# A hybrid encoder layer in split single precision: where the low halves of the weights, the scan's decay factors and a 64-row matmul are made

## The chip, the cores and the metric

One core of a Trainium2 chip runs the whole program. The metric is device time in microseconds (us) of one execution; of the kernel before there are three timed executions, and one more that carried a profile. TensorE is PE in the profile and its weight loads are PEld; VectorE is DVE, ScalarE is ACT, GpSimd is POOL, and SP is the engine that issues most transfers.

## What is computed

One layer of a streaming encoder on 544 tokens (512 of a prompt, 32 of a second request with caches), model width 1024:

```
h = rmsnorm(x); [q,k,v | z,xBC,dt | gate_a,gate_b] = h @ w_in
A: q, k normed per head; attention over a band with a clipped relative-position bias
B: xBC -> causal conv -> silu; chunked state-space scan (SSD) in 4 groups of 8 heads:
     seg   = acs[i] - acs[j]                  # acs: running sum of the decay exponents
     decay = exp(seg) for i >= j, else 0
     y     = ((C B^T) * decay) @ dx  +  (C @ h_prev) * exp(acs)
     h     = h_prev * exp(last)  +  B^T @ wj
   y -> gated rmsnorm with silu(z)
x += (sigmoid(gate_a) * (A @ w_proj_a) + sigmoid(gate_b) * (B @ w_proj_b)) @ w_out
x += down(gelu(conv(u_g)) * conv(u_v)),  u = rmsnorm(x) @ w_up
x += sigmoid(rmsnorm(x) @ w_ple_gate) * (p @ w_ple)
```

Outputs are y, the new keys and values, the scan's states and the conv contexts.

## The kernel before

All tokens lie along the free axis, features on the 128 partitions. A product with a weight matrix runs in units: one unit is a 128x1024 block of weights (128 output features, 8 chunks of 128 input features). `unit_order` lists 194 units in a fixed order: the conv and scan inputs and z first, then q, k, v, the gates, the projections, the feed-forward part and the last gate.

Each product is made in three passes of a fast reduced format (float32r). A weight tile is split as hi = rounded weight, lo = weight - hi; the activations likewise. `mm3` (L273) issues, for one chunk, hi x hi, hi x lo and lo x hi, each in two halves of 272 tokens: 6 matmuls a chunk, 48 a unit. One chunk is the grain in which the order of work on PE is written by hand: `dense.run(n)` puts n chunks between the pieces of the scan and of the attention. PE's instructions run in just the order in which the code issues them (each is pinned behind the last one); on the other engines a list scheduler fixes the order when the program is built, and each engine then runs its list in order.

Weights come by `load` (L234), two units (1 MB) in one transfer on SP's queue. `prep` (L240) makes hi on ACT (L250) and lo as a subtraction (L254): on DVE, but for units below 40 with an odd number on POOL. The code calls `prep` one unit ahead (PF = 1); hi and lo have two buffers each, so hi of unit u+1 can only be written when PE has finished unit u-1.

Three stages follow from this order. Up to about 395 us the conv inputs, z and the first q, k, v are made, with the scan between them: 20 iterations (4 groups, 5 chunks of tokens) of `ssd_a` (L611: products and decay factors) and `ssd_b` (L663: outputs and the next state). In `ssd_a` the decay factors of 8 heads are made in two halves: for each of 4 heads DVE computes min(ab - acs, 0) (L651), then ACT takes the exponential of all 4 (L652), then DVE multiplies with the masked product cbm (L653), which was copied from PSUM to SBUF (L625). From 395 to 645 us the attention of 8 pairs of heads runs between dense chunks. For a pair, `stack` (L806) builds ks (k rounded, twice, on 128 rows) and qs (q rounded on 64 rows, q's remainder on the other 64), and kl, the remainder of k on the head's own 64 rows; `att_a` (L823) adds up two products for the logits, the first on 128 rows (L848) and the second on the 64 rows of kl (L849). From 645 us on there is dense work alone, with its epilogues.

Of the kernel before, what the change touches and what calls it, by code (L numbers as in the profile page):

```python
# [9 lines left out]
F32 = mybir.dt.float32  # L10
# [106 lines left out]
def trunk(ctx: ExitStack, tc: tile.TileContext, a):  # L117
# [57 lines left out]
    def spt(shape, tag, bufs):  # L175
        return pools["sp"].tile(shape, F32, tag=tag, name=tag, bufs=bufs)
# [23 lines left out]
    r0 = wp.tile([128, 2, 1024], F32, tag="wr", name="wr", bufs=2)  # L200
    for k, c0, c1 in ((1, 0, 256), (2, 256, 512), (4, 512, 1024)):
        for u in range(2):
            nc.sync.dma_start(r0[:, u, c0:c1], a["w"][0, :, u, c0:c1])
        while len(xt) <= k:
            load_x(len(xt))
# [22 lines left out]
    raws = {0: r0}  # L228
# [3 lines left out]
    PF = 1  # L232

    def load(j):  # L234
        if 2 * j < len(order) and j not in raws:
            r = wp.tile([128, 2, 1024], F32, tag="wr", name="wr", bufs=2)
            nc.sync.dma_start(r, a["w"][j])
            raws[j] = r

    def prep(u):  # L240
        if u >= len(order) or u in ready or u in used:
            return
        load(u // 2)
        r = raws[u // 2][:, u % 2, :]
        hi = wp.tile([128, 1024], F32R, tag="wh", name="wh", bufs=2)
        lo = wp.tile([128, 1024], F32R, tag="wl", name="wl", bufs=2)
        ready[u] = (hi, lo)
        if u < 2:
            return r
        cp = S.copy(hi, r)  # L250
        if u == 3:
            tc.add_manual_dep(cp.ins, first_rstd[0].ins.name, ORDER, reason="order")
        eng = G if u < 40 and u % 2 == 1 else V
        eng.tensor_tensor(lo, r, hi.bitcast(F32), op=SUB)  # L254
        load(u // 2 + 1)
# [8 lines left out]
    def next_unit(kind, k0, c0):  # L264
        u = pos[0]
        assert order[u] == (kind, k0, c0), (order[u], kind, k0, c0)
        pos[0] += 1
        for i in range(u, u + PF + 1):
            prep(i)
        used.add(u)  # L270
        return ready.pop(u)
# [149 lines left out]
    load(1)  # L421
# [129 lines left out]
    def bias_vector():  # L551
        er = const.tile([16, EROW], F32, name="er")
        nc.sync.dma_start(er[:, 383:EROW], a["rb"])
        V.tensor_scalar(er[:, 383:EROW], er[:, 383:EROW], -1.0, None, op0=MUL)
        V.tensor_copy(er[:, 0:383], er[:, 383:384].to_broadcast([16, 383]))
        nc.sync.dma_start(evec, er)
        for h in range(16):
            dense.defer(16 + 16 * h, lambda h=h: bias_rows(h))
# [52 lines left out]
    def ssd_a(g, c):  # L611
# [12 lines left out]
        cbm = spt([128, 128], "cbm", 2)  # L624
        V.tensor_tensor(cbm[:Q, :Q], sm[:Q, 0:Q], tri[:Q, :Q], op=MUL)  # L625
# [18 lines left out]
        for hh in range(2):  # L644
# [4 lines left out]
            for i in range(4):  # L649
                hd = 8 * g + 4 * hh + i  # L650
                V.tensor_scalar(m[:Q, i, :Q], ab[:Q, i, :Q], tm[:Q, 1, c, hd : hd + 1], 0.0, op0=SUB, op1=MIN)  # L651
            S.activation(m[:Q, :, :Q], m[:Q, :, :Q], AF.Exp)  # L652
# [151 lines left out]
    stk = {}  # L804

    def stack(m, hi):  # L806
# [5 lines left out]
        kl = st(512, "kl") if hi == 0 else stk[0][2]  # L812
# [10 lines left out]
    def att_a(m, i):  # L823
# [15 lines left out]
        for hi in range(2):  # L839
# [3 lines left out]
            if i == 0:  # L843
                PE.matmul(L[:, :n], lhsT=q[own, 0:n], rhs=k[own, 0:n], start=True, stop=True)
            else:
                qs, ks, kl = stk[hi]
                sl = slice(n - 256, n - 128)
                PE.matmul(L[:, :n], lhsT=qs[:, sl], rhs=ks[:, 0:n], start=True, stop=False)  # L848
                PE.matmul(L[:, :n], lhsT=qs[own, sl], rhs=kl[own, 0:n], start=False, stop=True)  # L849
# [297 lines left out]
    prev = None  # L1147
    att_load(0)
# [115 lines left out]
```

## Time and profile before

| | us |
|---|---|
| three timed executions | 1412.04, 1412.58 (median), 1417.83 |
| the profiled execution, its own time | 1413.28 |
| its span in the trace | 1411.2 |
| PE busy | 1376.0 (98%) |
| DVE busy | 916.0 (65%) |
| ACT busy | 613.4 (43%) |
| POOL busy | 352.1 (25%) |

The median of the timed executions and the profiled one differ by 0.7 us. Matmuls are pipelined, so a matmul's own duration (about 290 ns for 272 tokens) is much longer than its distance to the next (about 125 ns); gaps on PE shorter than the difference do not show as idle time. The granted TensorE clock over the whole span was 0.991 of full speed.

The profile says by itself in which stages PE has room: the share of busy time over the whole span mixes a stage in which DVE is nearly full with 755 us in which only PE is.

### The profile page before, as it was taken

How to read it: one execution, taken by the hardware profiler on the slowest of the kernel's cores; microseconds unless marked ns; L12 is line 12 of the kernel's file. 1: busy time of each engine (PE TensorE's matmuls, PEld its weight loads, DVE VectorE, ACT ScalarE, POOL GpSimd, SP SyncE). 2: the span in 40 equal slices, each digit the busy share in tenths (PEclk: the TensorE clock that was granted, in tenths of full speed). 3: DMA queues.
4: the chain of work that ended last, by engine and by line, in shares of the span. 5: the costliest groups of instructions: out<-in, count | busy, mean ns of one | idle time of the engine just before them, and what ended most of it. 6: DMA issues, size and time to landing. Idle time of an engine off the chain costs nothing.

```text
span 1411.2 us, 26759 instructions
## 1 busy us (share of the span) xinstructions
PE 1376.0 (98%) x11065; PEld 1324.1 (94%) x11065; DVE 916.0 (65%) x1654; ACT 613.4 (43%) x1016; POOL 352.1 (25%) x464
## 2 busy tenths in 40 slices
PE   7998898989999999999999999999999999999998
PEld 7997897989988888889999999999999999999998
DVE  7999999996865555564355334577777537753545
ACT  5444343455566666654244223344444214432342
POOL 5466475464422112210000000023333103310000
PEclk9999999999999999999999999999999999999999
DMA  5723232323443323311222332222222232222221
GB/s 175 241 90 109 87 120 64 116 92 110 132 138 114 103 88 99 103 64 61 90 91 90 122 122 90 91 78 79 85 88 91 90 106 90 91 93 90 90 90 65
DMA packets 41929, 142.16 MB, mean 101 GB/s; under 512 B 9264, under 2 KB 13248, under 8 KB 29520
## 3 DMA queue, kind: packets, MB, share of 16 engines
q1 hardware_dynamic: 41808, 140.46, 29.6%
q8 instruction: 87, 1.43, 0.4%
q14 instruction: 34, 0.28, 0.1%
HBM read 129.27 MB, written 14.31 MB: 102 GB/s over the span
## 4 chain that ended last, share of the span: by engine, by line
PE 81%; DVE 13%; DMA 2%; ACT 2%; issue 1%; POOL 1%; SPq 0%; POOLq 0%; ACTq 0%
PE dps L130 72%; DVE m L651 3%; PE L L130 3%; DVE cv L597 2%; PE O L130 2%; DMA ab<-asc 2%; PE Tp L133 1%; DVE m L653 1%; DVE wl L254 1%; PE yps L130 1%; DVE xs L684 1%; DVE dx L636 1%; DVE wj L636 0%; PE qn L130 0%; DVE h L693 0%
## 5 line engine op out<-in xcount | busy, mean ns | idle before, releaser
L130 PE MATMUL dps<-hi,wh 128*128 128x272 f32 x2960 | 627.9, 294 | 14.9 <-DVE ext L572 14.6
L130 PE MATMUL dps<-lo,wh 128*128 128x272 f32 x2960 | 616.2, 290 | 5.3 <-DVE lo L375 5.3
L130 PE MATMUL dps<-hi,wl 128*128 128x272 f32 x2960 | 615.4, 290 | 2.3 <-DVE wl L254 1.9
L130 PEld LDWEIGHTS dps<-hi,wh 128*128 128x128 f32 x2960 | 467.4, 190 | 26.2 <-issue 18.5
L130 PEld LDWEIGHTS dps<-lo,wh 128*128 128x128 f32 x2960 | 469.0, 190 | 6.1 <-DVE lo L375 6.1
L130 PEld LDWEIGHTS dps<-hi,wl 128*128 128x128 f32 x2960 | 467.8, 189 | 3.1 <-DVE wl L254 2.5
L250 ACT CAST wh<-wr 128x1024 fp32r<-128x1024 f32 x192 | 201.2, 1048 | 379.3 <-PE dps L130 339.4
L254 DVE TENSOR_TENSOR wl<-wr,wh 128x1024 fp32r<-128x1024 f32 x173 | 213.3, 1233 | 48.2 <-ACT wh L250 43.3
L597 DVE SCALAR_TENSOR_TENSOR cv<-ext,hv,cv 128x547 f32<-128x547 f32 x72 | 76.9, 1068 | 2.7 <-ACT cv L594 2.1
L1021 DVE SCALAR_TENSOR_TENSOR ucv<-uext,vec,ucv 128x546 f32<-128x546 f32 x96 | 75.4, 785 | 4.2 <-ACT ucv L1018 2.4
L1014 POOL COPY cfo<-uext 128x2 f32<-128x2 f32 x48 | 10.4, 217 | 262.4 <-DVE uext L571 262.4
L1011 POOL MEMSET uext<- 128x2 f32 x48 | 4.6, 95 | 281.2 <-issue 281.2
L1053 DVE TENSOR_TENSOR x<-x,dps 128x544 f32<-128x544 f32 x24 | 17.3, 722 | 78.2 <-PE dps L130 78.0
L651 DVE TENSOR_SCALAR m<-ab,tm 128x128 f32<-128x128 f32 (+1 forms) x160 | 63.2, 452 | 5.3 <-DMA ab<-asc 5.3
L777 DVE CUSTOM_DVE_ANT_0 P<-L,bias 128x128 f32<-128x128 f32 (+3 forms) x64 | 30.9, 483 | 53.7 <-PE L L130 53.2
L569 DVE TENSOR_TENSOR uext<-dps,rstd 128x272 f32<-128x272 f32 x48 | 21.2, 442 | 63.1 <-PE dps L130 58.5
L254 POOL TENSOR_TENSOR wl<-wr,wh 128x1024 fp32r<-128x1024 f32 x19 | 50.8, 2672 | 44.8 <-ACT wh L250 36.8
L1015 POOL COPY cfo<-uext 128x2 f32<-128x2 f32 x48 | 55.5, 1157 | 0.0
L658 POOL TENSOR_TENSOR ab<-ab,bc 128x512 f32<-128x512 f32 (+1 forms) x32 | 42.5, 1332 | 40.1 <-ACT ab L657 37.8
L652 ACT ACTIVATE m<-m 128x512 f32<-128x512 f32 (+1 forms) x40 | 22.7, 567 | 65.8 <-DVE m L651 65.6
L733 POOL TENSOR_TENSOR ql<-qs,qh 128x544 fp32r<-128x544 f32 x16 | 22.0, 1376 | 103.6 <-ACT qh L732 91.6
L779 ACT ACTIVATE P<-P,sm 128x128 f32<-128x128 f32 (+3 forms) x64 | 36.0, 562 | 23.2 <-DVE sm L777 22.9
(246 smaller groups left out, 1626.4 us busy)
## 6 DMA issues: line engine op xcount, KB each, us to landing
wr<-in_w SPq DMA_DIRECT2D x96, 1024.0 KB, 4.9
ab<-asc SPq DMA_DIRECT2D x32, 256.0 KB, 5.5
bsc<-evec SPq DMA_DIRECT2D x16, 320.0 KB, 7.5
bias<-bsc SPq DMA_DIRECT2D x16, 256.0 KB, 3.5
xin<-in_xT SPq DMA_DIRECT2D x8, 272.0 KB, 5.4
out_o_v<-v SPq DMA_DIRECT2D x8, 272.0 KB, 2.1
out_o_k<-qk SPq DMA_DIRECT2D x8, 272.0 KB, 2.1
x<-in_xT SPq DMA_DIRECT2D x8, 272.0 KB, 4.6
```

The source lines that it names most:

```text
L130: return self._pin(nc.tensor.matmul(*args, **kw))
L250: cp = S.copy(hi, r)
L254: eng.tensor_tensor(lo, r, hi.bitcast(F32), op=SUB)
L597: V.scalar_tensor_tensor(y[:, :n], ext[:, j : j + n], hv[:, 24 * j + ti : 24 * j + ti + 1], y[:, :n], op0=MUL, op1=ADD)
L651: V.tensor_scalar(m[:Q, i, :Q], ab[:Q, i, :Q], tm[:Q, 1, c, hd : hd + 1], 0.0, op0=SUB, op1=MIN)
L652: S.activation(m[:Q, :, :Q], m[:Q, :, :Q], AF.Exp)
L658: G.tensor_tensor(ab[:, :, :Q], ab[:, :, :Q], cc[:, tk].unsqueeze(1).to_broadcast([128, 4, Q]), op=MUL)
L733: G.tensor_tensor(lo[:, :T], sq[:, :T], hi[:, :T].bitcast(F32), op=SUB)
L777: V.tensor_tensor_reduce(out=P, in0=L, in1=B, scale=1.0, scalar=3e38, op0=ADD, op1=MIN, accum_out=nm[:n])
L779: S.activation(P, P, AF.Exp, scale=-1.0, bias=nm[:n], accum_out=sm[:n])
L1015: G.tensor_copy(cfo[:, i, 2:4], ext[:, UW - 2 : UW])
L1021: V.scalar_tensor_tensor(y[:, :n], ext[:, j : j + n], vec[:, V_FW + 48 * j + i : V_FW + 48 * j + i + 1], y[:, :n], op0=MUL, op1=ADD)
```

## The change

Four edits, of which the first has several parts.

1. Units are loaded singly (512 KB). Units 0 to 5 are split as before, all of their subtractions on DVE. From unit 6 on, lo is first set to -hi (ACT for units below 40, DVE after), and then a transfer issued by POOL reads the same weights once more from memory and adds them onto lo. `prep` runs two units ahead, with three buffers of hi and of lo.
2. The decay factors: ACT computes relu(acs - ab) for each head, and the exponential takes a factor of -1. DVE's operation is gone. The masked product cbm stays in PSUM.
3. The second logits product has 128 rows: two tiles klz, zeroed once by POOL, hold the remainder of k on one half of the rows and zeros on the other.
4. The vector of biases is built in slots that are given back, and stored in two transfers.

```diff
-    PF = 1
-    def load(j):
-        if 2 * j < len(order) and j not in raws:
-            r = wp.tile([128, 2, 1024], F32, tag="wr", name="wr", bufs=2)
-            nc.sync.dma_start(r, a["w"][j])
+    PF = 2
+    def load(u):
+        if u < len(order) and u not in raws:
+            r = wp.tile([128, 1024], F32, tag="wr", name="wr", bufs=2)
+            nc.sync.dma_start(r, a["w"][u // 2, :, u % 2, :])
...
-        hi = wp.tile([128, 1024], F32R, tag="wh", name="wh", bufs=2)
-        lo = wp.tile([128, 1024], F32R, tag="wl", name="wl", bufs=2)
+        hi = wp.tile([128, 1024], F32R, tag="wh", name="wh", bufs=3)
+        lo = wp.tile([128, 1024], F32R, tag="wl", name="wl", bufs=3)
...
         cp = S.copy(hi, r)
-        eng = G if u < 40 and u % 2 == 1 else V
-        eng.tensor_tensor(lo, r, hi.bitcast(F32), op=SUB)
-        load(u // 2 + 1)
+        if u < 6:
+            V.tensor_tensor(lo, r, hi.bitcast(F32), op=SUB)
+        else:
+            if u < 40:
+                S.activation(lo, hi.bitcast(F32), AF.Copy, scale=-1.0)
+            else:
+                V.tensor_scalar(lo, hi.bitcast(F32), -1.0, None, op0=MUL)
+            G.dma_start(lo, a["w"][u // 2, :, u % 2, :], accum_op=ADD)
+        load(u + 1)
...
-        for i in range(u, u + PF + 1):
+        for i in range(u, u + (PF if u > 1 else 1) + 1):
...
-        er = const.tile([16, EROW], F32, name="er")
-        nc.sync.dma_start(er[:, 383:EROW], a["rb"])
...
-        nc.sync.dma_start(evec, er)
+        er, e0 = slot(name="er"), slot(name="e0")
+        nc.sync.dma_start(er[0:16, 0:257], a["rb"])
...
+        nc.sync.dma_start(evec[:, 0:383], e0[0:16, 0:383])
+        nc.sync.dma_start(evec[:, 383:EROW], er[0:16, 0:257])
+        done(er, e0)
...
-        cbm = spt([128, 128], "cbm", 2)
-        V.tensor_tensor(cbm[:Q, :Q], sm[:Q, 0:Q], tri[:Q, :Q], op=MUL)
+        cbm = sm[:, 0:128]
+        V.tensor_tensor(cbm[:Q, :Q], cbm[:Q, :Q], tri[:Q, :Q], op=MUL)
...
-                V.tensor_scalar(m[:Q, i, :Q], ab[:Q, i, :Q], tm[:Q, 1, c, hd : hd + 1], 0.0, op0=SUB, op1=MIN)
-            S.activation(m[:Q, :, :Q], m[:Q, :, :Q], AF.Exp)
+                S.activation(m[:Q, i, :Q], ab[:Q, i, :Q], AF.Relu, scale=-1.0, bias=tm[:Q, 1, c, hd : hd + 1])
+            S.activation(m[:Q, :, :Q], m[:Q, :, :Q], AF.Exp, scale=-1.0)
...
+    def lo_tiles():
+        for hi in range(2):
+            t = pools["ap"].tile([128, 512], F32R, tag=f"klz{hi}", name=f"klz{hi}", bufs=1)
+            G.memset(t.bitcast(F32), 0.0)
+            klz.append(t)
...
-        kl = st(512, "kl") if hi == 0 else stk[0][2]
+        kl = klz[hi]
...
-                PE.matmul(L[:, :n], lhsT=qs[own, sl], rhs=kl[own, 0:n], start=False, stop=True)
+                PE.matmul(L[:, :n], lhsT=qs[:, sl], rhs=kl[:, 0:n], start=False, stop=True)
```

The scheduler's lists show what moved. The first place is ACT's list in one iteration of the scan, from the copy of hi of a unit (wh) to that of the next; m and ab are the decay factors and their inputs, cv and th belong to the conv, bth and wjh to the state's product. Before:

```order
L250 CAST wh<-wr 128x1024
L652 ACTIVATE m<-m 128x512
L657 ACTIVATE ab<-ab 128x512
L594 ACTIVATE cv<-ext,hv 128x547
L652 ACTIVATE m<-m 128x512
L657 ACTIVATE ab<-ab 128x512
L627 CAST bth<-cbt 128x128
L250 CAST wh<-wr 128x1024
```

And in the same iteration of the changed kernel (L249 is the copy of hi, L256 the copy of -hi into wl, L658 the four relus):

```order
L249 CAST wh<-wr 128x1024
L659 ACTIVATE m<-m 128x512
L664 ACTIVATE ab<-ab 128x512
L658 ACTIVATE m<-ab,tm 128x128 x4
L601 ACTIVATE cv<-ext,hv 128x547
L256 ACTIVATE wl<-wh 128x1024
L659 ACTIVATE m<-m 128x512
L664 ACTIVATE ab<-ab 128x512
L634 CAST bth<-cbt 128x128
L647 CAST wjh<-wj 128x512
L249 CAST wh<-wr 128x1024
```

Between two copies of hi ACT now has four relus and one copy of -hi more; the copy of -hi stands some three instructions behind the hi that it reads.

The second place is POOL's list in the feed-forward part, where uext is a step's input to the conv and cfo the context that is kept. Before, one step and the start of the next:

```order
L1011 MEMSET uext 128x2
L1012 COPY uext<-ctx_f 128x2
L1014 COPY cfo<-uext 128x2
L1015 COPY cfo<-uext 128x2
L1011 MEMSET uext 128x2
```

And in the changed kernel, two whole steps (L259 is the adding transfer's issue, L1028 and L1029 the copies to cfo):

```order
L1025 MEMSET uext 128x2
L1026 COPY uext<-ctx_f 128x2
L1028 COPY cfo<-uext 128x2
L1029 COPY cfo<-uext 128x2
L1025 MEMSET uext 128x2
L1026 COPY uext<-ctx_f 128x2
L259 DMA wl<-in_w 128x1024
L1028 COPY cfo<-uext 128x2
L1029 COPY cfo<-uext 128x2
L259 DMA wl<-in_w 128x1024
```

A transfer is issued once a unit, and in every second step it stands behind the two copies to cfo and the preparation of the next uext.

## Rows read from the trace of the kernel before

**Rows 1.** The page, part 1: busy time, share of the span, instructions.

```profile
PE 1376.0 (98%) x11065; PEld 1324.1 (94%) x11065; DVE 916.0 (65%) x1654; ACT 613.4 (43%) x1016; POOL 352.1 (25%) x464
```

**Rows 2.** Stages; columns: PE, PEld, DVE, ACT, POOL busy, clock, DMA share, GB/s.

```profile
50.00:395.00 345.00, 321.91 (x2692) 304.11 (x2691) 319.46 (x631) 158.86 (x270) 187.48 (x181) 0.97 0.34 112
395.00:645.00 250.00, 249.63 (x2009) 218.67 (x2009) 140.01 (x352) 155.21 (x375) 46.65 (x45) 1.00 0.28 91
645.00:1400.00 755.00, 755.00 (x6007) 754.85 (x6007) 411.51 (x597) 272.26 (x334) 93.29 (x192) 1.00 0.27 92
```

**Rows 3.** The same view, 25 us inside the scan.

```profile
225.00:250.00 25.00, 19.30 (x149) 17.88 (x147) 24.03 (x52) 9.02 (x16) 12.91 (x18) 0.86 0.27 86
```

**Rows 4.** DVE groups, 50 to 395 us: count, busy us, mean ns, idle before.

```profile
L651 DVE TENSOR_SCALAR m<-ab,tm 128x128 f32<-128x128 f32 (+1 forms) x160 | 63.2, 452 | 5.3 <-DMA ab<-asc 5.3
L653 DVE TENSOR_TENSOR m<-m,cbm 128x512 f32<-128x512 f32 (+1 forms) x40 | 33.4, 838 | 2.3 <-ACT m L652 2.2
L254 DVE TENSOR_TENSOR wl<-wr,wh 128x1024 fp32r<-128x1024 f32 x22 | 28.3, 1288 | 1.0 <-ACT wh L250 0.8
...
L636 DVE TENSOR_TENSOR dx<-xst,tm 128x512 f32<-128x512 f32 (+1 forms) x20 | 13.5, 677 | 0.1
```

**Rows 5.** Who waited for whom, 50 to 395 us: total us, times, longest.

```profile
ACT m L652 <- DVE m L651: 65.6, 36, 4.4
...
PE dps L130 <- DVE ext L572: 14.2, 6, 4.4
```

**Rows 6.** ACT groups, 50 to 395 us.

```profile
L250 ACT CAST wh<-wr 128x1024 fp32r<-128x1024 f32 x39 | 40.6, 1042 | 12.7 <-PE dps L130 12.5
...
L744 ACT ACTIVATE qs<-qn,eps 128x272 f32<-128x272 f32 x12 | 5.1, 478 | 0.1
L627 ACT CAST bth<-cbt 128x128 fp32r<-128x128 f32 (+1 forms) x20 | 5.1, 256 | 14.2 <-DVE cbm L625 14.1
```

**Rows 7.** A POOL group, 50 to 395 us.

```profile
L254 POOL TENSOR_TENSOR wl<-wr,wh 128x1024 fp32r<-128x1024 f32 x17 | 44.5, 2617 | 31.3 <-ACT wh L250 23.3 <-DVE qr L728 8.0
```

**Rows 8.** PE in order of time, one step of attention: start us, us.

```profile
421.26 0.38 PE L130 MATMUL L<-ks,qs 128*128 128x256 f32 x1
421.57 0.38 PE L130 MATMUL L<-kl,qs 64*128 64x256 f32 x1
421.88 0.38 PE L130 MATMUL L<-ks,qs 128*128 128x256 f32 x1
422.19 0.39 PE L130 MATMUL L<-kl,qs 64*128 64x256 f32 x1
422.51 0.52 PE L130 MATMUL dps<-hi,wh 128*128 128x272 f32 x2
```

**Rows 9.** PEld groups by form, 395 to 645 us.

```profile
L130 PEld LDWEIGHTS L<-kl,qs 64*128 64x128 f32 x48 | 8.8, 183 | 8.9 <-issue 6.9
```

**Rows 10.** PE in order of time, the state's product in the scan.

```profile
140.84 0.39 PE L130 MATMUL st<-wjl,bth 128*128 128x512 f32 x1
141.08 0.39 PE L130 MATMUL st<-wjh,btl 128*128 128x512 f32 x1
```

**Rows 11.** Transfers: count, KB each, median us from issue to landing.

```profile
wr<-in_w SPq DMA_DIRECT2D x96, 1024.0 KB, 4.9
...
out_o_y<-x SPq DMA_DIRECT2D x7, 272.0 KB, 2.1
```

**Rows 12.** The line of the 1 MB weight loads, L237.

```profile
DMA to landing us min/median/max: 4.6/4.9/9.7
```

**Rows 13.** ACT in order of time, feed-forward part: one unit.

```profile
1194.58 1.05 ACT L250 CAST wh<-wr 128x1024 fp32r<-128x1024 f32 x1 [0.68 <-PE dps L130]
...
1200.62 1.05 ACT L250 CAST wh<-wr 128x1024 fp32r<-128x1024 f32 x1 [1.39 <-PE dps L130]
```

**Rows 14.** DVE in the same stretch.

```profile
1195.66 1.23 DVE L254 TENSOR_TENSOR wl<-wr,wh 128x1024 fp32r<-128x1024 f32 x1
```

**Rows 15.** POOL in the same stretch.

```profile
1195.61 0.18 POOL L1014 COPY cfo<-uext 128x2 f32<-128x2 f32 x1 [4.01 <-DVE uext L571]
1195.73 1.20 POOL L1015 COPY cfo<-uext 128x2 f32<-128x2 f32 x1
```

More of the change, by code (lines that the diff above doesn't have):

```diff
@@ L199, in trunk @@
     load_x(0)
-    r0 = wp.tile([128, 2, 1024], F32, tag="wr", name="wr", bufs=2)
+    raws = {u: wp.tile([128, 1024], F32, tag="wr", name="wr", bufs=2) for u in range(2)}
     for k, c0, c1 in ((1, 0, 256), (2, 256, 512), (4, 512, 1024)):
         for u in range(2):
-            nc.sync.dma_start(r0[:, u, c0:c1], a["w"][0, :, u, c0:c1])
+            nc.sync.dma_start(raws[u][:, c0:c1], a["w"][0, :, u, c0:c1])
         while len(xt) <= k:
@@ L225, in trunk @@
     done(wz_t)
-    raws = {0: r0}
     ready = {}
@@ L231, in trunk @@
     used = set()
-    PF = 1
-    def load(j):
-        if 2 * j < len(order) and j not in raws:
-            r = wp.tile([128, 2, 1024], F32, tag="wr", name="wr", bufs=2)
-            nc.sync.dma_start(r, a["w"][j])
-            raws[j] = r
+    PF = 2
[3 more added lines that the diff above has]
+            nc.sync.dma_start(r, a["w"][u // 2, :, u % 2, :])
+            raws[u] = r
     def prep(u):
@@ L242, in prep @@
             return
-        load(u // 2)
-        r = raws[u // 2][:, u % 2, :]
-        hi = wp.tile([128, 1024], F32R, tag="wh", name="wh", bufs=2)
-        lo = wp.tile([128, 1024], F32R, tag="wl", name="wl", bufs=2)
+        load(u)
+        r = raws[u]
+        hi = wp.tile([128, 1024], F32R, tag="wh", name="wh", bufs=3)
+        lo = wp.tile([128, 1024], F32R, tag="wl", name="wl", bufs=3)
         ready[u] = (hi, lo)
@@ L420, in trunk @@
                 prep_part(u, rw[u], (0, 256, 0, 512)[k], (256, 512, 0, 1024)[k])
-    load(1)
+    load(2)
     nc.sync.dma_start(hb, a["hb"].unsqueeze(0).to_broadcast([128, 2, 32]))
@@ L551, in bias_vector @@
     def bias_vector():
-        er = const.tile([16, EROW], F32, name="er")
-        nc.sync.dma_start(er[:, 383:EROW], a["rb"])
-        V.tensor_scalar(er[:, 383:EROW], er[:, 383:EROW], -1.0, None, op0=MUL)
-        V.tensor_copy(er[:, 0:383], er[:, 383:384].to_broadcast([16, 383]))
-        nc.sync.dma_start(evec, er)
+        er, e0 = slot(name="er"), slot(name="e0")
+        nc.sync.dma_start(er[0:16, 0:257], a["rb"])
+        V.tensor_scalar(er[0:16, 0:257], er[0:16, 0:257], -1.0, None, op0=MUL)
+        V.tensor_copy(e0[0:16, 0:383], er[0:16, 0:1].to_broadcast([16, 383]))
+        nc.sync.dma_start(evec[:, 0:383], e0[0:16, 0:383])
+        nc.sync.dma_start(evec[:, 383:EROW], er[0:16, 0:257])
+        done(er, e0)
         for h in range(16):
@@ L804, in trunk @@
     stk = {}
+    klz = []
+    def lo_tiles():
[3 more added lines that the diff above has]
+            klz.append(t)
     def stack(m, hi):
@@ L1147, in trunk @@
     prev = None
+    lo_tiles()
     att_load(0)
```

## The prediction

> **What bounds the kernel now.** I read the page's first part, then the busy time by stretches, then within each stage the groups, the waits and the timeline. The page says PE 98% busy [rows 1], which hides three different stages [rows 2]. From 645 to 1400 us PE has no gap: 6007 matmuls in 755 us, one every 125.7 ns, clock 1.00, with every other engine far from full (DVE 412 of 755). Nothing that eases DVE, ACT or POOL can shorten that stage. From 395 to 645 us PE is busy for 249.6 of 250, but its weight loads only 218.7: there the next weights aren't always loaded under the running matmul. In the scan, 50 to 395 us, DVE is busy for 319.5 of 345, PE for 321.9, ACT for 158.9, POOL for 187.5, and the clock is 0.97. That is the one stage that DVE limits: ACT's exponentials waited 65.6 us for DVE's min operations, and PE waited 14.2 us for a DVE eviction [rows 5]. A bad stretch shows how it costs twice: 225 to 250 us, PE busy for 19.3, granted clock 0.86 [rows 3], so part of it went at 1.2 instead of 2.4 GHz after PE had idled.
>
> What there is to win in the scan is then PE's idle time, 345 - 321.9 = 23.1 us, and the clock, 0.03 x 345 = 10.4 us: 33.5 us in all.
>
> **The change, part by part.**
>
> *Second logits product on 128 rows.* In a step the four logits matmuls and the dense one behind them start 0.31 us apart at 256 columns [rows 8]. Where rows don't change from 128 to 64 and back, 512 columns take 0.24 us [rows 10] and the dense 272 columns take 0.126 [rows 2]. On the line through these two, 256 columns would take 0.12, so each change costs 0.19 us. The weight loads agree: the 48 loads for kl have 8.9 us of idle time before them, 0.185 each [rows 9]. There are 8 pairs x 3 steps x 4 changes (ks to kl, kl to ks, ks to kl, kl to dense) = 96, and PE bounds this stage: 96 x 0.19 = 18 us. Between 0 (if something else than the row count makes the gap) and 18; I take 18, since dense work, 128 rows throughout, shows no such gap. The added rows multiply zeros and cost no columns. The two memsets and the remainder of k on POOL stand where POOL is busy for 46.7 of 250 us [rows 2].
>
> *Decay factors.* DVE loses 160 operations, 63.2 us [rows 4]. ACT gains 160 relus with a bias per row. A cast of 128 columns takes 256 ns, a function of 272 columns with such a bias 478 [rows 6]: between 41 and 76 us; nearer the first in size and the second in kind, I take 0.33 us each, 52 us. They stand ahead of the same exponential that waited for DVE. The Trainium skill, page "ScalarE: Activation LUTs", section "Rules for kernel authors", speaks against this edit: relu, min and their like belong on VectorE. By the price in the same page, about 280 + 0.833 x 128 = 387 ns for an operation with a bias per row (an estimate), ACT would gain 62 us rather than 52. The trace does not bear the rule out here: DVE's own operation on 128 columns takes 452 ns [rows 4], and DVE is the fuller engine.
>
> *cbm left in PSUM.* The multiplication L653 takes 838 ns with two operands in SBUF; L636, the same size with one operand in PSUM, takes 677 [rows 4]. 40 x 0.16 = 6.4 us less on DVE. Price: the PSUM buffer is held until the second multiplication, so a later PSUM product may wait for an eviction on DVE. Bounds: 0, and the whole 33.5 us again if DVE stays full; with DVE eased I take it as part of the third that I don't count below.
>
> *Low parts.* Of the 39 units split in the scan [rows 6], units 6 to 39 (34) lose a subtraction: 17 on POOL, 44.5 us [rows 7], and 17 of DVE's 22. The other 5 stay on DVE as a multiplication, taken as dear as the 1.29 us subtraction [rows 4]: DVE loses 17 x 1.29 = 22 us. ACT gains 34 copies of 1.04 us [rows 6], 35 us. POOL gains 34 issues; the trace has no transfer issued by POOL. Bounds: nothing, and a subtraction's 2.6 us [rows 7]; I take 1.2, the length of a short POOL instruction that DVE holds up [rows 15]: 41 us.
>
> Loads for the scan stage after the change: DVE 319.5 - 63.2 - 6.4 - 22 = 228, ACT 158.9 + 52 + 35 = 246, POOL 187.5 - 44.5 + 41 = 184, against 345 - 33.5 = 311 us that PE needs. No engine is full. The fullest is now ACT at 79%, and it runs in order: a copy of hi that waits for PE to leave a buffer holds the relus behind it, as the list shows. So I don't count all: two thirds of 33.5 us, 22 us. Bounds: 0 and 33.5.
>
> *The adding transfer's deadline.* In the dense stage a unit takes 6.04 us from one copy of hi to the next [rows 13]. hi of unit u+2 starts when PE leaves unit u-1; its low half is wanted when u+2 begins, 12.1 us later. In that time: hi 1.05, the negation on DVE where the subtraction now ends, 1195.66 + 1.23 - 1194.58 = 2.3 us after the start of hi [rows 13, 14]; POOL, in every second step, behind the two copies to cfo, which end 2.35 us after it [rows 15], and two short instructions, 2.6 us. That leaves 12.1 - 2.6 = 9.5 us from issue to landing. The trace has no adding transfer. It must read 512 KB of weights and 512 KB of lo and write the latter, so the nearest row is the 1 MB load: 4.9 us median, 9.7 at worst; the low bound is 2.1 us for a 272 KB store [rows 11, 12]. I take 5 to 6 us, in time with 3 us to spare, and count nothing; at 9.7 every unit would be 0.1 us late.
>
> *Rate.* The transfer engines are busy for 0.27 of the dense stage at 92 GB/s [rows 2]. Another 512 KB per 6.04 us, 87 GB/s, adds 0.25 if it moves like a plain load, 0.51 if it counts twice. They fill only beyond 0.73 / 0.25 = 2.9 times.
>
> *Other parts.* Single loads: twice as many issues on SP, which has nothing late. Bias vector: two small transfers instead of one, hidden by the scan. Units 3 and 5 move from POOL to DVE: 2.6 us, inside the scan's third. Dense stage: the negation replaces a subtraction on an engine busy for 412 of 755 us; cover remains.
>
> **Sum.** From the profiled execution, 1413.28 (span 1411.2, 2.1 us around it): 1413.3 - 18 - 22 = 1373 us. The median of the runs shown is 0.7 us lower than the profiled one, so 1373 or 1372; I say 1373, -2.8%.
>
> **The rivals.**
>
> A. *Low halves land late* (slower). Place: each unit of the dense stage, 755 / 6.04 = 125 of them. Price: if issue to landing takes X, two units take 2.6 + X, so a unit takes (2.6 + X) / 2 once X is over 9.5; or the engines fill at 2.9 times a plain load's time. At X = 11, 6.8 us, 0.76 us over: 95 us, giving 1373 + 95 = 1468. It outweighs the 40 us won from X = 10.1 on. For it: a kind of transfer that no row shows, weights read twice, and a worst plain landing of 9.7 [rows 12]. Against: the median of 4.9, with half of the time to spare. The Trainium skill, page "SBUF — State Buffer", section "Who interferes with whom", adds a reason for it: POOL writes the descriptors of its own transfers, and is locked out while DVE runs an operation of one source at double rate from both ports, so the transfer looks slow. The row nearest to it is the 2-element copy that took 1.20 us beside a DVE operation, its twin before it 0.18 [rows 15]: 1 us more of delay, not enough to reach 9.5 by itself.
>
> B. *The scan's stalls stay*: ACT, at 79% and in order, or the PSUM buffer, takes DVE's place. Then only the logits' 18 us are won: 1395. For it: hi's copies waited 12.5 us for PE [rows 6], with the relus now behind them. Against: no engine is above 80%.
>
> C. *The row count is not what makes the gaps between logits matmuls* (the edit doesn't do what it says): 1413 - 22 = 1391. Against it: gaps stand just where the row count changes.
>
> D. *B and C together*: 1413, no change.
>
> **How the numbers follow.** Forecast 0.50 (its own range 1361 to 1387: the scan gives between all and a quarter of 33.5 us); A 0.19; B 0.15; C 0.10; D 0.06. A difference of 0.5%, 7 us, is about what a measurement can tell. Faster: forecast, B and C, 0.75. Within 0.5%: D and a landing at just X = 10.1, 0.07. Slower: the rest of A, 0.18. The range leaves out A and about 0.02 below: 1356 is the logits' 18 and all of the scan's 33.5 us, with 6 for what the view of idle time hides; 1414 is D.
>
> **What the profile after would show.** Right: in the scan DVE falls from 93% to about 73% and ACT rises to about 79%, PE's idle time there falls below 10 us and the clock is 0.99 or more; logits matmuls of 256 columns start 0.12 us apart; the dense stage keeps one matmul every 125.7 ns; adding transfers land 5 to 6 us after issue; the transfer engines are at 0.5 to 0.8 there. Wrong: PE waiting for wl in the dense stage (A); PE waiting for the exponentials, an eviction or a PSUM buffer in the scan (B); gaps of 0.19 us that stay (C).

## The result, and the profile after

The changed kernel takes 1380.92 us (median of 4 runs, 1379.06 to 1382.47) where the kernel before takes 1412.94: a ratio of 0.9766, interval 0.9739 to 0.9793, 32 us less. Forecast were 1373 us, 40 less. The profiled execution took 1382.47 us.

The page of the changed kernel, part 1, answers to [rows 1]; then the three stages by their new ends, which answer to [rows 2], with the same columns.

```profile
PE 1354.3 (98%) x11065; PEld 1320.3 (96%) x11065; DVE 756.0 (55%) x1479; ACT 684.0 (50%) x1210; POOL 403.5 (29%) x635
```

```profile
50.00:375.00 325.00, 313.92 (x2657) 299.02 (x2659) 224.43 (x444) 227.63 (x453) 153.58 (x205) 0.97 0.72 170
375.00:615.00 240.00, 238.41 (x2070) 222.63 (x2060) 138.18 (x364) 157.83 (x385) 69.08 (x73) 1.00 0.70 160
615.00:1370.00 755.00, 755.00 (x6011) 754.85 (x6010) 350.69 (x596) 271.62 (x331) 161.16 (x316) 1.00 0.83 178
```

PE runs the same 11065 instructions in the same order in both, so stages can be cut at an instruction. Three marks from the view of a tile (count, ns min/median/max, first and last start in us): the first product of B and C (cbt), which opens the scan; the first logits of the 32 sampled columns, which open the attention stage; the last product with the values, which closes it. Before:

```profile
L130 PE MATMUL cbt<-bc x40: 196/272/347, 74.3 to 361.0; 128*128 128x128 f32 x32, 128*32 128x32 f32 x8
L130 PE MATMUL L<-qk x32: 272/323/374, 391.0 to 604.8; 64*128 64x128 f32 x32
L130 PE MATMUL O<-PT,vt x320: 272/273/324, 401.0 to 644.3; 128*64 128x128 f32 x160
```

After:

```profile
L130 PE MATMUL cbt<-bc x40: 196/272/275, 76.2 to 346.1; 128*128 128x128 f32 x32, 128*32 128x32 f32 x8
L130 PE MATMUL L<-qk x32: 272/322/373, 377.0 to 576.8; 64*128 64x128 f32 x32
L130 PE MATMUL O<-PT,vt x320: 272/273/324, 386.0 to 613.9; 128*64 128x128 f32 x160
```

So the start is 1.9 us longer (76.2 against 74.3), the scan 15.9 shorter (300.8 against 316.7), the attention stage 16.4 shorter (236.9 against 253.3), and the dense stage the same: 30.4 us less at its first matmul, as at the last. The forecast had 0, 22, 18 and 0.

In the attention stage the step of [rows 8] now reads, in order of time:

```profile
382.11 0.39 PE L130 MATMUL L<-ks,qs 128*128 128x256 f32 x1
382.33 0.28 PE L130 MATMUL L<-klz,qs 128*128 128x256 f32 x1
382.45 0.28 PE L130 MATMUL L<-ks,qs 128*128 128x256 f32 x1
382.57 0.28 PE L130 MATMUL L<-klz,qs 128*128 128x256 f32 x1
382.69 0.41 PE L130 MATMUL dps<-hi,wh 128*128 128x272 f32 x2
```

Three of the four distances fell from 0.31 to 0.12 us, as forecast; the first only to 0.22 (why is not known). Over 24 steps that is 24 x (3 x 0.19 + 0.09) = 15.8 us of the 16.4. The steps of 384 and 512 columns behave alike: all 96 distances of the trace sum to 35.6 us before and to 19.2 after.

The transfers: queues with packets, MB and share of the 16 engines; loads with their median to landing; and the adding transfer's line.

```profile
q0 software_dynamic: 27072, 98.58, 43.9%
q1 hardware_dynamic: 55664, 140.46, 32.8%
...
wr<-in_w SPq DMA_DIRECT2D x192, 512.0 KB, 4.3
wl<-in_w POOLq DMA_DIRECT2D x188, 512.0 KB, 7.1
```

```profile
DMA to landing us min/median/max: 5.4/7.1/10.3
```

Low parts land in 7.1 us at the median, later than the 5 to 6 forecast. In the dense stage the slowest takes 8.6 us, within the 9.5 allowed (the 10.3 is in the scan), and PE has no gap there.

In the scan, who waited for whom, where [rows 5] showed DVE twice:

```profile
ACT m L658 <- DMA ab<-asc: 41.1, 17, 5.8
DVE m L660 <- ACT m L659: 38.6, 20, 4.8
...
PE xst L133 <- DVE xs L691: 5.5, 2, 2.9
...
PE qn L130 <- POOL ql L740: 2.4, 2, 2.1
```

The exponentials no longer wait for DVE. Their relus now wait for ab, the loaded rows of decay sums, which the min operations on DVE had waited for only 5.3 us [rows 4]. PE, which had waited most for DVE's eviction ext [rows 5], waits elsewhere: for DVE's eviction of y before it transposes xs, and for POOL's remainder of q. Two stretches are still slow, 150 to 175 and 225 to 250 us, the second answering to [rows 3]:

```profile
150.00:175.00 25.00, 22.45 (x169) 21.36 (x168) 17.09 (x39) 14.45 (x34) 6.97 (x13) 0.86 0.73 163
225.00:250.00 25.00, 22.10 (x165) 21.00 (x164) 20.01 (x48) 17.39 (x39) 9.58 (x19) 0.86 0.65 148
```

### The profile page after: what moved, and what is told of

Read it like the earlier page. It is cut to its first block, busy times and chain, and to the rows that moved or that the text cites. A ratio compares the mean times of both kernels' runs of the same rounds, so it can differ in the third digit from the quotient of the medians.

```text
span 1380.8 us, 27400 instructions
## 1 busy us (share of the span) xinstructions
PE 1354.3 (98%) x11065; PEld 1320.3 (96%) x11065; DVE 756.0 (55%) x1479; ACT 684.0 (50%) x1210; POOL 403.5 (29%) x635
## 3 DMA queue, kind: packets, MB, share of 16 engines
q0 software_dynamic: 27072, 98.58, 43.9%
q1 hardware_dynamic: 55664, 140.46, 32.8%
## 4 chain that ended last, share of the span: by engine, by line
PE 80%; ACT 6%; DVE 6%; DMA 5%; issue 2%; POOL 1%; SPq 0%; ACTq 0%; DVEq 0%; POOLq 0%
PE dps L130 72%; DMA ab<-asc 4%; DVE cv L604 2%; PE O L130 2%; PE L L130 2%; ACT m L658 2%; PE Tp L133 1%; DMA wr<-in_w 1%; ACT wh L249 1%; PE yps L130 1%; DVE qs L833 1%; ACT m L659 1%; ACT wl L256 0%; PE gps L130 0%; DVE m L660 0%
## 5 line engine op out<-in xcount | busy, mean ns | idle before, releaser
L249 ACT CAST wh<-wr 128x1024 fp32r<-128x1024 f32 x192 | 201.1, 1048 | 372.3 <-PE dps L130 306.2
L259 POOL DMA_DIRECT2D wl<-in_w x188 | 163.5, 870 | 625.7 <-DVE wl L258 330.4
L258 DVE TENSOR_SCALAR wl<-wh 128x1024 fp32r<-128x1024 f32 x154 | 109.0, 708 | 51.6 <-ACT wh L249 46.9
L658 ACT ACTIVATE m<-ab,tm 128x128 f32<-128x128 f32 (+1 forms) x160 | 48.7, 372 | 41.1 <-DMA ab<-asc 41.1
L1028 POOL COPY cfo<-uext 128x2 f32<-128x2 f32 x48 | 10.3, 214 | 168.7 <-DVE uext L578 168.7
L660 DVE TENSOR_TENSOR m<-m,cbt 128x512 f32<-128x512 f32 (+1 forms) x40 | 24.0, 601 | 42.3 <-ACT m L659 38.6
L1032 ACT ACTIVATE ucv<-uext,vec 128x546 f32<-128x546 f32 x48 | 40.6, 846 | 7.2 <-DVE uext L579 2.2
L373 ACT CAST hi<-me 128x544 fp32r<-128x544 f32 x24 | 15.5, 647 | 57.7 <-DVE me L1053 57.7
L665 POOL TENSOR_TENSOR ab<-ab,bc 128x512 f32<-128x512 f32 (+1 forms) x32 | 36.7, 1161 | 23.9 <-ACT ab L664 23.8
L946 DVE TENSOR_TENSOR g<-dps,rstd 128x544 f32<-128x544 f32 x16 | 11.6, 723 | 47.9 <-PE dps L130 47.9
```

The lines of the kernel that those rows point to most:

```text
L258: V.tensor_scalar(lo, hi.bitcast(F32), -1.0, None, op0=MUL)
L259: G.dma_start(lo, a["w"][u // 2, :, u % 2, :], accum_op=ADD)
L658: S.activation(m[:Q, i, :Q], ab[:Q, i, :Q], AF.Relu, scale=-1.0, bias=tm[:Q, 1, c, hd : hd + 1])
L660: V.tensor_tensor(m[:Q, :, :Q], m[:Q, :, :Q], cbm[:Q, :Q].unsqueeze(1).to_broadcast([Q, 4, Q]), op=MUL)
L665: G.tensor_tensor(ab[:, :, :Q], ab[:, :, :Q], cc[:, tk].unsqueeze(1).to_broadcast([128, 4, Q]), op=MUL)
L1032: S.activation(y[:, :n], ext[:, 0:n], AF.Identity, scale=vec[:, V_FW + i : V_FW + i + 1], bias=vec[:, V_FB + i : V_FB + i + 1])
```

## The experiments

The first row and the second are the comparison above. Ratios are to the kernel before, timed beside each version on the same chip (its medians there: 1415.1 to 1415.7 us, against 1412.94 in the first comparison; the changed kernel was not timed again beside the later versions). Stage lengths are cut at the three marks above, in one profiled execution of each. They scatter by 2 to 3 us: the start, which the changed kernel shares with low parts alone, cbm in SBUF and state scaling on DVE, took 76.2, 78.1, 78.2 and 78.8 us.

| kernel | median us | ratio, interval | start | scan | attention |
|---|---|---|---|---|---|
| before | 1412.94 | | 74.3 | 316.7 | 253.3 |
| changed | 1380.92 | 0.9766, 0.9739 to 0.9793 | 76.2 | 300.8 | 236.9 |
| rows alone | 1400.61 | 0.9895, 0.9879 to 0.9911 | 74.3 | 316.8 | 236.9 |
| decay alone | 1385.97 | 0.9797, 0.9780 to 0.9813 | 74.9 | 292.0 | 253.1 |
| low parts alone | 1398.66 | 0.9882, 0.9866 to 0.9898 | 78.1 | 300.8 | 253.1 |
| changed, cbm in SBUF | 1380.65 | 0.9760, 0.9741 to 0.9780 | 78.2 | 300.7 | 236.9 |
| rows and decay | 1372.23 | 0.9688, 0.9669 to 0.9708 | 76.4 | 286.8 | 236.9 |
| changed, subtraction in the scan | 1379.43 | 0.9744, 0.9723 to 0.9764 | 78.0 | 294.3 | 236.9 |
| changed, state scaling on DVE | 1378.83 | 0.9742, 0.9720 to 0.9765 | 78.8 | 291.9 | 240.8 |
| subtraction in the scan, one ahead | 1379.27 | 0.9744, 0.9728 to 0.9759 | 78.7 | 293.8 | 237.0 |
| changed, three loads | 1377.94 | 0.9742, 0.9719 to 0.9766 | 73.6 | 298.6 | 236.9 |
| rows, decay, single loads | 1371.37 | 0.9687, 0.9673 to 0.9701 | 74.7 | 290.8 | 236.9 |

### Each part alone

Each is the kernel before with one part of the change: the logits' part (klz, and `qs[:, sl]`, `kl[:, 0:n]` in place of the halves); the decay's part (relu on ScalarE, `cbm = sm[:, 0:128]`); all that belongs to the low parts (adding transfer, loads of single units, three buffers, two units ahead, bias vector).

> The kernel before with the second logits product on 128 rows and nothing else. Theory (a change of the row count between two matmuls costs 0.19 us, 96 of them): in the attention stage 256-column logits start 0.12 us apart, the stage is 16 to 18 us shorter, scan and dense stage as before: 1395 to 1397 us. Rival (part of the gain seen in the changed kernel's attention stage comes from the weights' low parts, which leave POOL free there): only 8 to 12 us of it, 1401 to 1405.

> The kernel before with the decay factors on ScalarE and cbm left in PSUM, and nothing else. DVE loses about 70 us in the scan, ACT gains about 49. Theory D (the scan is limited by DVE's load, three quarters of its relief is here): three quarters or more of the 16 us that the scan lost, -12 to -16: 1397 to 1401 us. Rival (the low parts' relief of DVE and POOL at the places where the units' evictions wait is what counts): -4 or less, 1409 or more.

> The kernel before with the weights' low parts by the adding transfer (from unit 6), single loads, three buffers and the bias vector's two stores, and nothing else. Theory D: DVE loses 22 us of its 319 in the scan, a quarter of all relief, so the scan gains 3 to 5 us; the start loses 2 us (units 3 and 5 subtracted on DVE instead of POOL): 1409 to 1412 us, dense stage unchanged at 125.7 ns a matmul. Rival (the transfers' load costs elsewhere: decay loads land later while DVE is still full): 1415 to 1420.

The rows gave what the theory said: 16.4 us in the attention stage, as much as in the changed kernel, and nothing elsewhere. By the medians it is 14.5 us, beside a kernel before that ran 2 us slower here than in the first comparison; that lies between the two expectations, and it is the stage's length that rules the rival out.

Decay alone gave 29 us (24.7 in the scan), twice what was expected, and low parts alone 16.5 (15.9 in the scan, 3.8 lost at the start) where 1 to 4 were expected. Both expectations took the gain as proportional to DVE's relief; that fell. Either relief removes the same long stalls: PE's waits for DVE's eviction ext, 14.2 us before [rows 5], are gone with decay alone and 3.2 us with low parts alone:

```profile
PE dps L130 <- DVE ext L579: 3.2, 2, 2.1
```

The three parts sum to 60 us; together they gave 32. Rows and scan touch different stages and must add up, so the loss lies between decay and low parts: with both, the scan takes 300.8 us, with decay alone 292.0.

### Without the adding transfers

```diff
 rows and decay = the kernel before, with
+        cbm = sm[:, 0:128]
...
+                S.activation(m[:Q, i, :Q], ab[:Q, i, :Q], AF.Relu, scale=-1.0, bias=tm[:Q, 1, c, hd : hd + 1])
...
+                PE.matmul(L[:, :n], lhsT=qs[:, sl], rhs=kl[:, 0:n], start=False, stop=True)
```

> The kernel before with the 128-row logits product, the decay factors on ScalarE and cbm in PSUM, but with the low parts by subtraction, loads of two units and two buffers as before. Theory A (the adding transfers take back in the scan what the decay factors win: alone these gave 29 us, all three edits together 34, the rows 15 of them): the two parts add up, 1386 - 15 = 1371 us, 10 us less than the changed kernel. Rival (two parts share one gain whatever the low parts do): 1379 to 1383, as the changed kernel.

1372.23 us: the two parts add up, and this version beats the changed kernel; the intervals, 0.9669 to 0.9708 and 0.9739 to 0.9793, do not touch. In the profiled execution the scan is 29.9 us shorter than before, nearly all of the 33.5 that the prediction found there. What belongs to the low parts costs 9 us on top of that by the medians, 11 by the ratios. The view by stages, 50 us to its scan's end:

```profile
50.00:365.00 315.00, 311.83 (x2694) 298.12 (x2693) 258.56 (x472) 201.28 (x426) 182.85 (x190) 0.99 0.38 124
```

PE idles 3.2 us and the clock is 0.99 although DVE is at 82%; in the changed kernel it is at 69% and PE idles 11.1. DVE's load is no longer what counts.

### cbm in SBUF, and the state's scaling on DVE

```diff
 changed, cbm in SBUF
-        cbm = sm[:, 0:128]
-        V.tensor_tensor(cbm[:Q, :Q], cbm[:Q, :Q], tri[:Q, :Q], op=MUL)
+        cbm = spt([128, 128], "cbm", 2)
+        V.tensor_tensor(cbm[:Q, :Q], sm[:Q, 0:Q], tri[:Q, :Q], op=MUL)

 changed, state scaling on DVE
-            G.tensor_tensor(hn.rearrange(...
+            V.tensor_tensor(hn.rearrange(...
```

> The changed kernel with cbm written to SBUF again, as before. Theory H (the PSUM buffer held until the second multiplication makes the transposes of xs wait, 2.8 us at 154 us and 3.2 us at 229 us, and the granted clock of 0.86 around them follows): both waits fall under 1 us, the clock there rises to 0.95 or more, DVE gains 6 us that it can carry: 1372 to 1376 us. Rival Q (these waits are DVE's queue: the eviction of y stands behind three convolution steps and a wait for tanh): both waits stay within 1 us, DVE is busy for 6 us more: 1380 to 1384 us.

The time is the rival's, 1380.65; the places are the theory's. Before xs is transposed PE no longer waits; it waits for DVE 28 matmuls later instead. The waits of 153 to 166 us, first in the changed kernel, then with cbm in SBUF:

```profile
PE xst L133 <- DVE xs L691: 2.5, 1, 2.5
```

```profile
PE dps L130 <- DVE ext L579: 3.2, 1, 3.2
```

Holding the PSUM buffer moved a stall and made none: behind both stands the same late DVE.

> The changed kernel with the scaling of the state (h times el, 16 operations of 128x512) on DVE instead of POOL. In the changed kernel two convolution steps on DVE take 5.7 us instead of 0.8, at 139 and 215 us, both beside an issue of the adding transfer on POOL and four POOL operations run back to back right behind it. Theory S (DVE waits while POOL's two-operand operations run without a gap; they run so because POOL stood at the issue): with two of the four gone both steps take under 3.5 us, the waits of the transposes of xs (2.8 and 3.2 us) shrink under 1.5 and the granted clock of 0.86 there is 0.93 or more: 1372 to 1377 us. Rival T (the issue itself holds DVE up): both steps stay over 5 us, DVE is 11 us busier: 1380 to 1385.

DVE was late because one convolution step took 5.73 us instead of 0.79. DVE and POOL of the changed kernel, in order of time:

```profile
139.27 5.73 DVE L604 SCALAR_TENSOR_TENSOR cv<-ext,hv,cv 128x547 f32<-128x547 f32 x1 [0.44 <-ACT cv L601]
144.92 0.68 DVE L660 TENSOR_TENSOR m<-m,cbt 128x512 f32<-128x512 f32 x1
```

```profile
138.79 0.89 POOL L259 DMA_DIRECT2D wl<-in_w  x1 [1.52 <-ACT wl L256]
139.41 2.35 POOL L698 TENSOR_TENSOR h<-h,el 128x512 f32<-128x512 f32 x2
141.42 1.58 POOL L665 TENSOR_TENSOR ab<-ab,bc 128x512 f32<-128x512 f32 x1
142.64 0.39 POOL L594 MEMSET ext<- 128x3 f32 x1
142.69 0.47 POOL L595 COPY ext<-ctx_s 128x3 f32<-128x3 f32 x1
142.83 1.57 POOL L665 TENSOR_TENSOR ab<-ab,bc 128x512 f32<-128x512 f32 x1
```

The step ends 0.6 us after POOL's row, as the other one, at 215 us, does. With the two scalings (L698) on DVE the longest of the 72 steps is 2.6 us; the line of that code in the changed kernel, then here:

```profile
L604 DVE SCALAR_TENSOR_TENSOR cv<-ext,hv,cv x72: 687/789/5727, 32.0 to 253.7; 128x547 f32<-128x547 f32 x72
```

```profile
L604 DVE SCALAR_TENSOR_TENSOR cv<-ext,hv,cv x72: 691/789/2614, 31.1 to 249.6; 128x547 f32<-128x547 f32 x72
```

A step beside an issue alone (142 us, in this version) took its usual 0.79 us. So theory S holds for the steps: it is POOL's row, not the issue. (Why POOL's operations stood in a row is not shown.) The first wait before xs went and the clock of 150 to 175 us rose to 0.93; the second wait stayed at 2.2 us, behind three steps in a row. The scan is 8.9 us shorter than the changed kernel's, but the start is 2.6 longer and the attention stage 3.9 (its first product with the values waits 2.3 us for ScalarE). The median, 1378.83, lies between the two expectations, and its interval overlaps the changed kernel's: what the steps are worth in the whole is not settled. Two versions of the next part, without adding transfers before 331 us, have no step over 2.8 us and still take 1379.

### Where the 9 us go

```diff
 changed, subtraction in the scan
-        if u < 6:
-            V.tensor_tensor(lo, r, hi.bitcast(F32), op=SUB)
-        else:
-            if u < 40:
-                S.activation(lo, hi.bitcast(F32), AF.Copy, scale=-1.0)
-            else:
-                V.tensor_scalar(...)
-            G.dma_start(lo, ..., accum_op=ADD)
+        if u < 40:
+            (G if u % 2 else V).tensor_tensor(lo, r, hi.bitcast(F32), op=SUB)
+        else:
+            V.tensor_scalar(...)
+            G.dma_start(lo, ..., accum_op=ADD)
 the same, one ahead
-        for i in range(u, u + (PF if u > 1 else 1) + 1):
+        for i in range(u, u + (PF if u > 38 else 1) + 1):
 rows, decay, single loads: the same again, with subtraction for all units and
-    PF = 2        wh, wl: bufs=3
+    PF = 1        wh, wl: bufs=2
```

> The changed kernel with the low parts of units 6 to 39, those of the scan stage, by subtraction on POOL and DVE in turn, as before; single loads and three buffers, and the adding transfers of the later units, stay. Theory A1 (it is the negation, the issue and the landing in the scan that take back): the scan as with the decay factors alone, only the start still 2 us longer: 1372 to 1375 us. Rival A2 (the single loads with 512 KB less ahead and the broader bias stores at the start do it): 1378 or more. Either way the dense stage at 125.7 ns a matmul.

> The kernel with subtraction in the scan and adding transfers from unit 40 on (1379 us), with one unit instead of two prepared ahead until unit 38. Theory P (what takes back is the preparing of two units ahead: copies and splits of unit u+2 stand in ACT's, DVE's and POOL's order ahead of work that PE wants sooner, and at the start ACT stands at a copy whose load has not landed): the waits of 3.5 us at 45 us and of 2.1 to 2.8 us for POOL's remainder of q fall under 0.5 us: 1370 to 1374 us, as without any adding transfer. Rival L (single loads, 512 KB instead of 1 MB ahead, and the bias stores): 1377 to 1381.

> The kernel with the rows and decay edits and no adding transfers (1372 us), with nothing else added than the loads of single units (two buffers of 512 KB instead of two of 1 MB) and the bias vector's two stores; low parts by subtraction, two buffers for the parts, one unit ahead, as before. Theory L2 (ACT and DVE run in order and stand at a copy whose load was issued late, behind the bias stores; later the shorter row of loads shifts the splits against PE's wants): the wait of 3.5 to 4 us at 45 us is there, and 1376 to 1381 us. Rival B (the third buffer for the parts, and the transfers behind it, are what costs): the wait at the start stays under 1 us or is all that stays: 1371 to 1375.

In the first two the theories missed, and the times were those of the rivals: with no adding transfer before 331 us, and with one unit ahead, it stays 1379 us. So the negation, the issue and the landing up to there, and the preparing of two units, are at most 1 or 2 of the 9 us by the medians and 3 of 11 by the ratios, whose intervals overlap (the scans of the profiled executions differ by 6.5 to 7; the changed kernel's was the slowest of its runs). The third, with single loads and bias stores alone, is 1371.37: those cost nothing, so the rivals' cause, theory L2 here, is out too.

Between the last two (0.9728 to 0.9759 and 0.9673 to 0.9701) stand the third buffer for the high and low parts and, from unit 39 on, the second unit ahead and the adding transfers. The first of these transfers is issued at 331.4 us; up to there the third buffer is all that differs in the code. PE runs the same list in both, so the two profiled executions can be laid side by side: the one with the third buffer is 4.0 us behind at the start of the scan, 7.0 at the matmul that stands at 152.4 us in the one and at 145.4 in the other, 8.3 at 161 and 5.0 at 331. The last 2.0 of the 7.0 us that remain to the end come between 340 and 350 us, behind the first transfers. PE waits there for POOL's remainder of q (ql), which stands behind the second issue; in the version without transfers it does not wait there:

```profile
345.61 0.87 POOL L256 DMA_DIRECT2D wl<-in_w  x1
346.22 1.64 POOL L737 TENSOR_TENSOR ql<-qs,qh 128x544 fp32r<-128x544 f32 x1
```

```profile
PE qn L130 <- POOL ql L737: 2.1, 1, 2.1
```

So the larger part, 5 of 7 us, is the third buffer's, as far as one execution of each can tell. The table agrees: the scan starts at 76.2 to 78.8 us in the six versions with three such buffers and two for raw weights, and at 74.3 to 76.4 in the five with two. No run has the third buffer without the later transfers.

How it costs is seen at the start. The waits of 25 to 50 us and ACT in order of time with the third buffer (one ahead):

```profile
ACT wh L249 <- DMA wr<-in_w: 4.5, 1, 4.5
PEld dps L130 <- ACT th L604: 4.0, 1, 4.0
DVE dtt L512 <- ACT dtt L502: 4.0, 1, 4.0
```

```profile
35.22 0.84 ACT L598 ACTIVATE cv<-ext,hv 128x547 f32<-128x547 f32 x1 [0.16 <-DVE ext L576]
40.53 1.05 ACT L249 CAST wh<-wr 128x1024 fp32r<-128x1024 f32 x1 [4.47 <-DMA wr<-in_w]
41.48 0.33 ACT L502 ACTIVATE dtt<-dtt 128x160 f32<-128x160 f32 x1
```

The same place with two buffers:

```profile
35.59 0.85 ACT L595 ACTIVATE cv<-ext,hv 128x547 f32<-128x547 f32 x1 [0.16 <-DVE ext L573]
36.34 1.03 ACT L249 CAST wh<-wr 128x1024 fp32r<-128x1024 f32 x1
38.40 0.34 ACT L499 ACTIVATE dtt<-dtt 128x160 f32<-128x160 f32 x1 [1.03 <-DVE dtt L498]
```

With two buffers a copy waits until PE leaves a buffer, which kept it behind its load. With three that wait is gone, the copies run through the two raw buffers one unit ahead, and in the place where unit 4's copy stood unit 5's now stands, at a load issued 4 us later (32.0 instead of 28.4) that shares the queues with 320 KB bias stores. ACT runs in order: dt's exponentials stand behind the copy, DVE's next step behind them, the eviction that PE wants behind that. The changed kernel has the same wait: ACT for wr 3.0 us, PE 2.0 for the eviction.

> The changed kernel with three buffers of raw weights instead of two, loads issued two units ahead. Theory P: only the wait for a load at the start (2.2 us at 45 us) goes, 1 to 3 us: 1378 to 1380 us. Rival L (the short row of loads is the cause everywhere): 1371 to 1375.

```diff
-    raws ... tag="wr", name="wr", bufs=2
+    raws ... tag="wr", name="wr", bufs=3
         load(u + 1)
+        load(u + 2)
```

A third raw buffer takes that wait away: the start is 73.6 us instead of 76.2, PE waits there for nothing over 0.3. The time falls by about that, 1377.94, as theory P said, though the interval overlaps. The other 3 us that the pair above differs by at 152 us were not taken apart. With the third buffer the granted clock is 0.96 and 0.97 from 75 to 125 us against 1.00 with two, but rows and decay, with two buffers as well, has 0.93 and 1.00 there, so the clock is no mark of the third buffer. PE waits 1.1 us for an eviction at 136 that it doesn't wait for with two.

### The deadline and the load on the transfers

```diff
 two buffers
-    PF = 2        wh, wl: bufs=3
+    PF = 1        wh, wl: bufs=2
 more traffic, in load(u)
+            if u >= 64:
+                nc.sync.dma_start(wp.tile([128, 1024], F32, tag="wx", name="wx", bufs=1), a["w"][u // 2, :, u % 2, :])
```

> The changed kernel with two buffers instead of three for the high and the low parts, and one unit instead of two prepared ahead: the deadline of rival A is then missed. Theory (a unit takes negation and issue delay, 2.6 us, and the landing, 7.1, once these exceed its 6.04 us of matmuls): 9.7 us a unit in the dense stage, 3.7 late in each of 125, 460 us more there and some 100 in the stages before, perhaps more where the clock falls: 1840 to 2000 us. Rival (the transfer is faster when nothing else is under way, as PE's waits thin out the loads): 5 us to land, 7.6 us a unit, 1600 us.

1677.42 us in its one execution: neither. The landing stayed at 6.9 us, against the rival, and the theory's price was too high: 77 units in the 600 us from 900 on, 7.8 us each, not 9.7.

```profile
900.00:1500.00 600.00, 503.42 (x3704) 491.05 (x3703) 243.59 (x442) 171.12 (x203) 120.75 (x269) 0.95 0.64 138
```

The sum had an error. From the start of one hi copy to the first use of that low half pass about 9.75 us (copy at 1019.37, use at 1029.10). They hold one whole unit D, the next unit's first four matmuls (0.5) and its wait D - 6.04: so 2D - 5.54 = 9.75, D = 7.65. The prediction's rival A made the same error with three buffers: two whole units and a wait, 3D - 5.54 = 2.6 + X, so at X = 11 a unit takes 6.38 us and the loss is 0.34 x 125 = 43 us, not 95.

> The changed kernel with each unit's weights of the attention's end and the dense stage (unit 64 on) loaded once more into a tile that nobody reads: another 512 KB per 6.04 us on top of a busy share of 0.83. By the shares of before and after (0.27 for one plain load, 0.83 with an adding one more) another plain load adds 0.27: over 1. Theory F (a share of 0.83 means that the engines are nearly full): they can't carry it, low parts land later than the 9 to 10 us that are allowed, a unit takes 6.4 us or more: 1420 or more. Rival (the share counts waiting for each other's packets, there is room): share 0.9 to 1, low parts land in 8 to 9 us, no matmul waits: 1379 to 1384.

1538.12 us in its one execution, but not the test that was meant: since nobody reads the extra tile, its 130 loads were issued as soon as each could be, between 18 and 740 us, in scan and attention. The dense stage behind them ran without a gap. The scan and its relus' first wait:

```profile
50.00:480.00 430.00, 358.29 (x2732) 332.14 (x2730) 220.26 (x460) 232.17 (x464) 157.01 (x211) 0.88 0.84 231
```

```profile
ACT m L660 <- DMA ab<-asc: 145.1, 35, 11.4
```

The relus wait 145.1 us for ab instead of 41.1, and PE idles 72 of 430 us. The traffic itself is the smaller part of that: with the engines at 0.84 and 231 GB/s, ab lands 6.7 us after its issue at the median instead of 5.6, 1.1 us more for each of 40 loads. What weighs more, by that sum, is that ab was issued late. The loads of ab and of the weights are issued from one queue, SP's, in order, and between 50 and 480 us SP stood for 302 us (75 waits) at the extra loads, each of which waits until the one before has landed in the tile's only buffer. So the run tells little of what the scan pays for traffic, and whether the dense stage would bear more stays open.

## Why the prediction was right, and where it was not

**Second logits product.** Right: the row count makes the gaps, and the edit gives the same 16.4 us alone and with the others, against 18 forecast. What is left of the 18 is the first distance of each step, 0.22 instead of 0.12.

**Loads in the scan.** Well sized: DVE 224 (forecast 228), ACT 228 (246), POOL 154 (184). A relu takes 372 ns (330 taken), 48.7 us in all (52). A second multiplication by cbm takes 601 ns (677). An issue on POOL is 0.88 us (1.2).

**Two thirds of 33.5 us.** This is the step that was mis-sized: the scan and the start gave 15.9 - 1.9 = 14 us, not 22. The caution was right, its reason only in part. ACT's copies of hi still wait for PE, 9.3 us in the scan (12.5 before), but where PE then stood idle for work behind a copy, at the start, that copy waited for a load. Relief of DVE by the decay edit alone gives nearly all of the 33.5 (rows and decay: 29.9 in the scan). The forecast "PE idle there below 10 us, clock 0.99" held for that kernel, 3.2 us and 0.99, and not for the changed one, 11.1 and 0.97.

**Low parts.** The step failed in sign: counted as a part of the relief, they take 9 us back beside the decay edit, which had already made that relief. The prediction used the third buffer for the deadline alone and did not ask which waits it lets go, and what then stands in ACT's order. That the total still fell into the range is in part luck: the third that was held back for an in-order ACT, and was not needed for the decay edit, paid for a cost that the sum did not have.

**cbm in PSUM.** Its price was put inside the uncounted third; the experiment shows it at zero. The stall that the buffer takes over was there anyway.

**Adding transfer.** In time, as forecast, though slower (7.1 us), and the engines fuller: 0.83 where 0.5 to 0.8 was written. Per byte the software queue, which carries the adding transfers, holds the engines 1.9 times as long as the hardware queue with the plain ones (43.9% for 98.58 MB, 32.8% for 140.46). The Trainium skill, page "Collectives: The Full Stack", section "The bandwidth ceiling: the fold count and why AG ≠ RS ≠ AR", tells of reduce-scatter that its add reads two sources, with two descriptors for each piece, and that all-gather, a plain copy, ran 1.93 times as fast. The two figures agree; that the cause is the same here no run shows. Rival A did not occur; its price was more than doubled by the error above.

**Rivals B, C, D.** C and D are out with the rows alone. B happened in a small way: new waits (for a load at the start, for DVE's eviction of y behind POOL's row, for POOL's remainder of q) took the place of some of the old ones, and 8 of the 40 us did not come.

## What to carry to other kernels

Ask of one more buffer not only what it lets start earlier, but which in-order engine then stands at something that the old wait kept it behind. When two edits relieve the same engine, the second is worth only what the first has left, and costs its full price: time each part alone and in pairs. Cut stages at instructions of the bounding engine that both kernels share, and follow the difference through the whole stage before it is given to one cause: shares of busy time say only that DVE was relieved, not which edit won by it.

## What the runs showed of the hardware

- A DVE operation of 0.79 us with two SBUF inputs took 5.73 us while POOL ran a row of operations without a pause, and ended with that row. The Trainium skill, page "SBUF — State Buffer", section "Who interferes with whom", says that a DVE instruction with two SBUF inputs contends with a GpSimd instruction that reads SBUF, since they share a port pair that works as an exclusive lock. The trace agrees, and shows how long it can last: DVE's operation ended 0.6 us after four two-input operations of POOL, not after the first of them.
- The busy share of the transfer engines is no measure of bytes: 0.83 at 178 GB/s with adding transfers, 0.84 at 231 GB/s with more plain loads among them.
- Where the row count changes between 128 and 64, the next matmul starts 0.19 us later; without the change the distance of 256 columns is 0.12 us (the first of each step 0.22).
